# A hybrid mixer: one half of a convolution a step later, a gate product in its old place, and three small sums further back on VectorE

## The chip, the cores and the metric

The kernel runs on one core of a Trainium2 chip. The metric is the device time of one execution in microseconds (us). Three timed executions of the kernel before gave 1531.76, 1535.86 and 1537.22 us; their median, 1535.86 us, is the time before. The profiled execution took 1536.88 us, of which the span from the first to the last instruction is 1535.1 us.

## The reference

The network has two layers over 128 context tokens and 256 latent tokens of width 1024. Each layer is a half-step SwiGLU network, a token mixer, and a second half-step SwiGLU network, each with adaptive shift, scale and gate and a layer norm behind it. The mixer has one input projection and one output projection, and between them three head groups side by side:

```python
z = h @ p["w_in"]
zq, zi, zff, zfb, zg, zglu, cq, ck, cv = jnp.split(z, cuts, axis=-1)
o_fw, s_fw = _hgrn_scan(qa, k_fw, ia, logf_fw, s0[:, 0])            # linear recurrence, forward
o_bw, s_bw = _hgrn_scan(rev(qa), rev(k_bw), rev(ia), rev(logf_bw), s0[:, 1])
o_a = _rms_norm(o_fw + rev(o_bw), g) * jax.nn.silu(zg)              # gated by zg
u = _depthwise_conv(glu_a * jax.nn.sigmoid(glu_b), conv_w, conv_b)  # 31 taps, 256 channels
o_conv = jax.nn.silu(_layer_norm(u, conv_ln_g, conv_ln_b))
kc = _rms_norm(ck, p["k_norm_g"])                                   # keys, then rotary for latents
o_c = _block_attention(qc, kc, vc)
y = jnp.concatenate([o_a, o_conv, o_c], axis=-1) @ p["w_out"]
```

All of it is fp32. The change touches three things of the mixer: the depthwise convolution, the product that gives `zg`, and the sums of squares in the keys' RMS norm.

## The kernel before, in words

The 384 tokens are three blocks (`tok` 0 is the context, 1 and 2 are the latents). The order of instructions on TensorE (PE), VectorE (DVE), ScalarE (ACT) and GpSimd (POOL) is the order in which the Python code is written (`manual_schedule`); each engine works its own list in order and waits at an instruction whose input is not there. There is no planner around the change; DMAs are issued by SyncE (SP), in order too.

The change lies in the loop `for i in range(2 * NT + 1)` of `mixer` (seven steps, `i` = 0 to 6), which runs once a layer. Its pieces are these:

- `scores(i)`: 64 small matmuls (32x32 and 64x64 tiles, L1195) for one pair of heads and one token block, into one of two PSUM pairs, and then four masked copies on VectorE (`copy_predicated`, L1204) that put them into the tiles `A1[i % 2]` and `A2[i % 2]`.
- `outputs(i - 1)`: the matmuls that read those tiles (L1229). For token blocks 1 and 2 two groups on carried states come first; then the group on `A2`, which needs the second masked copy, and then the group on `A1`, which needs the fourth.
- `conv(ct)`: half of the channels of the convolution, 32 matmuls in the code and 64 records in the trace (L1004), and ScalarE's evacuation (L1012). `CONV_AT` says at which step each half stands.
- `zg(n)`: the gate's projection for one token block, 24 matmuls of 128x256 (L664) from `W[14]` and `W[15]`, and a ScalarE copy. `HFILL` says at which step the first one stands; the other two stand in the attention loop behind.
- In step 0, `prep(14)` and `prep(15)` split two weight tiles (ScalarE cast L888, VectorE subtraction L894). In steps 0 and 1, `dec[1].level(32)` and `level(64)` work on decay tiles (L1118 to L1125).
- `head_ssq` (L931 to L938): a ScalarE square, a VectorE sum (L932) and two GpSimd instructions; three calls for the keys, whose result is read by `norm_rope` (L948 to L956) in steps 2, 3 and 4.
- In step 4, behind the second half of the convolution, `wo_prep(4)` and `wo_prep(5)` split weights of the output projection (L600, L601). In step 6 `keys_turn` transposes the keys (L1420), after `norm_rope` of token block 2, and `att(0)` begins the attention (L1445).

Of the kernel before, what the change touches and what calls it, by code (L numbers as in the profile page):

```python
# [18 lines left out]
P = 128  # L19
DM = 1024  # L20
KT = 8
NT = 3
# [11 lines left out]
]  # L34
NA = len(ATT_ORDER)
UW, UC, OW = 432, 428, 399
CONV_AT = {2: 0, 4: 1}
MH = 4
TMID = 2
FILL = (-1, 1, 2)  # L40
HFILL = (5,)
SLOW, FAST, LAST = [2, 2, 2, 2], [3, 2, 3], [3, 3, 1, 1]


class Net:
# [810 lines left out]
    def mixer(self, l, eps, nxt):  # L856
# [12 lines left out]
        mp = scope(es, "mix")  # L869
# [29 lines left out]
        def prep(n, eng, pool=None):  # L899
            lo(n, hi(n, pool))  # L900
# [11 lines left out]
        kn = self.t(mp, [P, NT, P], "kn")  # L912
# [14 lines left out]
        def head_ssq(x, nh, t1):  # L927

            f = 64 if nh == 8 else 1
            ss = self.t(mp, [P, 16], "ss", bufs=8)  # L930
            nc.scalar.activation(t1, x, AF.Square)  # L931
            nc.vector.reduce_sum(  # L932
                ss[:, 0:nh], t1.rearrange("p (h d) -> p h d", d=64), axis=AX.X
            )
            nc.gpsimd.tensor_scalar(
                ss[:, 0:nh], ss[:, 0:nh], f / 64, f * 1e-6, ALU.mult, ALU.add
            )
            nc.gpsimd.tensor_tensor(  # L938
                ss[:, 8 : 8 + nh], ss[:, 0:nh], self.eps[:, 2:3].to_broadcast([P, nh]), ALU.pow
            )  # L940
            return ss
# [191 lines left out]
        def state_turn(p):  # L1133
            pt = self.wbank()
            for i, (d, tok) in enumerate(((0, 0), (0, 1), (1, 0), (1, 2))):
                nc.tensor.transpose(
                    pt[:, i * P : (i + 1) * P],
                    dec[p].Kc[d][:, tok * P : (tok + 1) * P],
                    self.ident,
                )  # L1140
            kN = self.t(hp, [P, 4, P], "kN")
            nc.scalar.copy(kN.rearrange("p a b -> p (a b)"), pt)
            return kN

        def states(p, kN):
            pt = self.wbank()
            for i, tok in enumerate((0, 1, 0, 2)):
                for hh in range(2):
                    rs = slice(64 * hh, 64 * hh + 64)
                    nc.tensor.matmul(  # L1150
                        pt[rs, i * 64 : i * 64 + 64],
                        kN[:, i, rs],
                        vN[:, tok, 128 * p + 64 * hh : 128 * p + 64 * hh + 64],
                        start=True,
                        stop=True,
                    )
            S1 = self.t(hp, [P, 4, 64], "S1", bufs=2)
            for i, d in ((0, 0), (2, 1)):
                nc.scalar.copy(S1[:, i, :], pt[:, i * 64 : i * 64 + 64])
                nc.sync.dma_start(  # L1160
                    self.o["new_state_hgrn"][0, l, d, 2 * p : 2 * p + 2].rearrange(
                        "h d e -> (h d) e"
                    ),
                    S1[:, i, :],
                )
            for i, d in ((1, 0), (3, 1)):
                nc.vector.scalar_tensor_tensor(
                    S1[:, i, :], S0[:, d, p, :], dec[p].et[d][:, d + 1 : d + 2],
                    pt[:, i * 64 : i * 64 + 64], ALU.mult, ALU.add,
                )  # L1170
            return S1
# [3 lines left out]
        def scores(i):  # L1175

            p, tok = divmod(i, NT)
            Qd, Kd, lev = dec[p].D, dec[p].K, dec[p].lev  # L1180
            tsl = slice(tok * P, (tok + 1) * P)
            a1, a2 = A1[i % 2], A2[i % 2]
            prs = [(Qd[0], Kd[0], a1), (Qd[1], Kd[1], a2)] + [(q_, k_, a1) for q_, k_ in lev]
            if i < 2:
                sbs[i] = self.pair(1 + i)
            sb = sbs[i % 2]
            for kd_, m, x in ((0, 32, 0), (1, 32, 0), (2, 32, 0), (3, 32, 0), (4, 32, 32), (5, 64, 64)):
                n = min(kd_, 3)
                if i < 2 and n < 3:
                    m = P  # L1190
                for hh in range(2):
                    rs = slice(64 * hh, 64 * hh + 64)
                    for c in range(0, P, m):
                        r = c ^ x
                        nc.tensor.matmul(  # L1195
                            sb[c : c + m, hh, n * P + r : n * P + r + m],
                            prs[kd_][1][rs, tok * P + c : tok * P + c + m],
                            prs[kd_][0][rs, tok * P + r : tok * P + r + m],
                            start=True,
                            stop=True,  # L1200
                            tile_position=(64 * hh, c),
                        )
            for n in range(4):
                nc.vector.copy_predicated(  # L1204
                    prs[n][2],
                    self.smask[:, n, :].unsqueeze(1).to_broadcast([P, 2, P]),
                    sb[:, :, n * P : (n + 1) * P],
                )
# [141 lines left out]
        k_ss = []  # L1350
# [35 lines left out]
        glu(1)  # L1386
        S1s = [states(0, kN)]
        dec[1].level(16)
        for tok in range(NT):
            k_ss.append(head_ssq(kn[:, tok, :], 2, self.t(mp, [P, P], "t1k", bufs=2)))  # L1390
        nc.sync.dma_start(self.o["new_cache_v"][0, l].rearrange("s h d -> s (h d)"), kv[:, 0, :])

        wop, wraw = {}, {}
# [2 lines left out]
        def wo_load(kb):  # L1396
            raw = wraw[kb] = self.t(self.rawp, [P, 2, DM], "raw")
            if kb < 4:
                nc.sync.dma_start(
                    raw, wo[l, kb * P : (kb + 2) * P, :].rearrange("(k p) n -> p k n", p=P)  # L1400
                )
            else:
                for g in range(2):
                    r0 = 512 + g * 256 + (kb - 4) * 64
                    nc.sync.dma_start(
                        raw[64 * g : 64 * g + 64],
                        wo[l, r0 : r0 + 128, :].rearrange("(j p) n -> p j n", p=64),
                    )

        def wo_prep(k, pool, tag, size=2 * DM, lo=nc.vector):  # L1410
            w = self.t(pool, [P, size], tag, F32R)[:, 0 : 2 * DM]
            w = w.rearrange("p (a n) -> p a n", a=2)
            wop[k] = self.split_to(w, wraw[k // 2 * 2][:, k % 2, :], lo)
# [3 lines left out]
        def keys_turn():  # L1417
            pt = self.wbank()
            for i, src in enumerate((kn[:, 0, :], ck[:, 0, :], kn[:, 1, :], kn[:, 2, :])):
                nc.tensor.transpose(pt[:, i * P : (i + 1) * P], src, self.ident)  # L1420
            nc.scalar.copy(kT.rearrange("p a b -> p (a b)"), pt)
# [93 lines left out]
        def att(n):  # L1515
            units.append(Att(n))
            units[n].scores()

        for i in range(2 * NT + 1):
            if i < 2 * NT:  # L1520
                scores(i)
            if i == NT + 1:
                S1s.append(states(1, kN))
            if i == NT:
                kN = state_turn(1)
            if i == 2 * NT:
                keys_turn()
            if i == 0:
                prep(14, nc.vector)
                prep(15, nc.vector)  # L1530
            if i == 2:
                wo_load(4)
            if i in CONV_AT:
                conv(CONV_AT[i])
            if i == 5:
                wo_load(6)
                wo_load(0)
                wo_load(2)
            if i == 4:
                wo_prep(4, self.wgu, "wgu")  # L1540
                wo_prep(5, self.wgu, "wgu")
            if i > 0:
                outputs(i - 1)
            if i in HFILL:
                zg(HFILL.index(i))
            if i == NT + 1:
                o_turn(0)
            if i == 2 * NT:
                att(0)
                units[0].exp()  # L1550
            if i == NT:
                es1.close()
                ap_ = scope(es, "at")
                gh = self.t(ap_, [P, 1, 256], "gh")
                nc.sync.dma_start(
                    gh[:, 0, :], a["hgrn_norm_g"][l : l + 1, :].to_broadcast([P, 256])
                )
            if i < 2:
                dec[1].level(32 << i)
            elif i < 2 + NT:  # L1560
                tok = i - 2
                norm_rope(
                    kn[:, tok, :], k_ss[tok], tok, 2, 1, self.t(mp, [P, P], "t1k", bufs=2)
                )
# [233 lines left out]
```

## Time and profile before

| what | value |
|---|---|
| median of three timed executions | 1535.86 us |
| profiled execution, its own time | 1536.88 us |
| span of the profiled execution | 1535.1 us |
| TensorE matmuls busy | 1508.9 us (98%) |
| VectorE, ScalarE, GpSimd busy | 1058.8, 649.2, 59.2 us |
| mean granted TensorE clock | 0.993 |

Busy times are of one engine each and overlap. A busy TensorE says that matmuls are in flight, not that they run at their best pace; the granted clock says how much of the full 2.4 GHz the engine got. The chain of waits walks back from the last instruction to whatever released it, so its pieces add up to the span, where the busy times do not.

### The profile page before, as it was taken

To read this page: it belongs to the slowest core of one execution; us is meant where nothing else is said; L and a number is where in the kernel's file an instruction comes from. 1 tells how busy PE (TensorE), PEld (TensorE's weight loads), DVE (VectorE), ACT (ScalarE), POOL (GpSimd) and SP (SyncE) were. 2 spreads that over 40 slices of the span, in tenths; PEclk is the share of its full clock that TensorE was granted. 3 is DMA by queue.
4 is the path that set the end of the run, shared out by engine and by line. 5 is a ranking of instruction groups with operands and counts; after the bars stand their busy time and mean duration, and the time that the engine had idled before them with its cause. 6 is when DMAs were issued, how large, how long until landed. Compare 5 with 4: busy or idle time off the path is not lost.

```text
span 1535.1 us, 23662 instructions
## 1 busy us (share of the span) xinstructions
PE 1508.9 (98%) x9605; PEld 1343.1 (87%) x9605; DVE 1058.8 (69%) x1525; ACT 649.2 (42%) x1112; POOL 59.2 (4%) x96
## 2 busy tenths in 40 slices
PE   8999999999999999999999999999999999999997
PEld 7889999989677899999989999998986789999996
DVE  4788878679667777777676676675795786554334
ACT  3434333367475533333353333333773764332331
POOL 0000000030101000000000000000210100000001
PEclk9999999999999999999999999999999999999998
DMA  9886766423524466666535565642335146342411
GB/s 385 307 292 227 243 233 222 176 67 134 125 83 165 165 225 230 231 221 211 201 114 216 168 244 192 220 164 112 118 102 160 48 168 248 127 179 110 165 55 41
DMA packets 63940, 272.27 MB, mean 177 GB/s; under 512 B 9224, under 2 KB 13784, under 8 KB 48984
## 3 DMA queue, kind: packets, MB, share of 16 engines
q1 hardware_dynamic: 63832, 270.77, 49.8%
q8 instruction: 75, 1.23, 0.3%
q14 instruction: 33, 0.27, 0.1%
HBM read 267.71 MB, written 3.03 MB: 176 GB/s over the span
## 4 chain that ended last, share of the span: by engine, by line
PE 92%; ACT 2%; DVE 2%; DMA 2%; issue 1%; SPq 0%; POOL 0%; DVEq 0%; POOLq 0%; ACTq 0%
PE w L610 45%; PE d L623 26%; PE d L683 7%; PE d L610 4%; PE w L1004 2%; PE w L664 1%; PE w L208 1%; PE d L1195 1%; PE w L427 1%; PE d L1229 1%; ACT Pr L1463 1%; DVE G L196 1%; PE d L1445 1%; PE d L1493 1%; DMA wi<-ffn_w_in_first 1%
## 5 line engine op out<-in xcount | busy, mean ns | idle before, releaser
L610 PE MATMUL w<-xh,wgu 128*128 128x384 f32 x2720 | 711.6, 337 | 1.4 <-DVE hf L777 1.4
L610 PEld LDWEIGHTS w<-xh,wgu 128*128 128x128 f32 x2720 | 494.0, 188 | 10.9 <-issue 4.9
L610 PE MATMUL w<-xl,wgu 128*128 128x384 f32 x1360 | 455.7, 335 | 0.0
L623 PE MATMUL d<-wo,hh 128*128 128x512 f32 x1056 | 284.4, 391 | 1.5 <-DVE hf L777 1.5
L196 DVE SCALAR_TENSOR_TENSOR G<-t,cc,G 128x1024 f32<-128x1024 f32 x224 | 272.9, 1280 | 0.0
L610 PEld LDWEIGHTS w<-xl,wgu 128*128 128x128 f32 x1360 | 256.3, 188 | 2.2
L623 PEld LDWEIGHTS d<-wo,hh 128*128 128x128 f32 x1056 | 196.8, 188 | 38.4 <-DVE hf L777 1.9
L601 DVE TENSOR_TENSOR wgu<-raw,wgu 128x1024 fp32r<-128x1024 f32 x166 | 196.1, 1222 | 39.1 <-ACT wgu L600 38.6
L779 ACT CAST hh<-hf 128x384 fp32r<-128x384 f32 x82 | 42.1, 514 | 343.4 <-DVE hf L777 343.4
L777 DVE TENSOR_TENSOR hf<-w,sg 128x384 f32<-128x384 f32 x79 | 44.0, 557 | 182.6 <-PE w L610 182.6
L600 ACT CAST wgu<-raw 128x1024 fp32r<-128x1024 f32 x166 | 166.2, 1049 | 3.4 <-DMA raw<-ffn_w_in 3.4
L623 PE MATMUL d<-wo,hl 128*128 128x512 f32 x528 | 163.2, 390 | 0.0
L775 ACT ACTIVATE sg<-w 128x384 f32<-128x384 f32 x79 | 38.8, 491 | 264.2 <-PE w L610 264.2
L623 PEld LDWEIGHTS d<-wo,hl 128*128 128x128 f32 x528 | 99.1, 188 | 21.2
L601 DVE TENSOR_TENSOR wo<-raw,wo 128x1024 fp32r<-128x1024 f32 x90 | 109.7, 1219 | 10.9 <-ACT wo L600 10.9
L683 PE MATMUL d<-wgu,xh 128*128 128x512 f32 x336 | 104.6, 392 | 0.0
L600 ACT CAST wo<-raw 128x1024 fp32r<-128x1024 f32 x90 | 94.4, 1049 | 11.7 <-DMA raw<-ffn_w_out 11.3
L780 DVE TENSOR_TENSOR hl<-hf,hh 128x384 fp32r<-128x384 f32 x82 | 45.8, 559 | 47.6 <-ACT hh L779 47.6
L683 PEld LDWEIGHTS d<-wgu,xh 128*128 128x128 f32 x336 | 62.3, 188 | 12.5
L683 PE MATMUL d<-wgu,xl 128*128 128x512 f32 x168 | 65.6, 390 | 0.0
L436 ACT ACTIVATE t<-w,colB,colA 128x128 f32<-128x128 f32 x120 | 43.6, 469 | 46.3 <-PE w L427 38.7
L486 POOL TENSOR_TENSOR st<-st,eps 128x1 f32<-128x1 f32 x18 | 8.0, 445 | 1202.0 <-ACT X L482 1202.0
(279 smaller groups left out, 1513.7 us busy)
## 6 DMA issues: line engine op xcount, KB each, us to landing
raw<-ffn_w_in SPq DMA_DIRECT2D x80, 1024.0 KB
t<-w_mod SPq DMA_DIRECT2D x128, 512.0 KB
raw<-ffn_w_out SPq DMA_DIRECT2D x44, 1024.0 KB
raw<-w_in SPq DMA_DIRECT2D x12, 1024.0 KB
raw<-entry SPq DMA_DIRECT2D x10, 1024.0 KB
raw<-w_mod_first SPq DMA_DIRECT2D x8, 1024.0 KB
G<-gates SPq DMA_DIRECT2D x12, 512.0 KB
raw<-w_in_vk SPq DMA_DIRECT2D x4, 1024.0 KB
```

Source lines behind the costliest of these rows:

```text
L196: nc.vector.scalar_tensor_tensor(ac, raw, cc, ac, ALU.mult, ALU.add)
L436: self.nc.scalar.activation(m[:, k, :], pts[k // 4][:, k % 4 * P : (k % 4 + 1) * P], AF.Identity, scale=A[:, k, c : c + 1], bias=B[:, k, c ...
L600: nc.scalar.copy(w[:, 0], src)
L601: lo_engine.tensor_tensor(w[:, 1], src, w[:, 0].bitcast(F32), ALU.subtract)
L610: nc.tensor.matmul(ps, w[:, wi, k, :], x[:, k, :], start=(k == 0 and i == 0), stop=(k == KT - 1 and i == 2),)
L623: nc.tensor.matmul(acc[:, n, :], h, w[:, wi, n * 512 : n * 512 + 512], start=(first and i == 0), stop=(last and i == 2),)
L683: self.nc.tensor.matmul(ps, x[:, k, tok * P : (tok + 1) * P], w[k // 2][:, wi, k % 2, :], start=(k == 0 and i == 0), stop=(k == KT - 1 and ...
L775: nc.scalar.activation(sg, pg, AF.Silu)
L777: nc.vector.tensor_mul(hf, pu, sg)
L779: nc.scalar.copy(hh, hf)
L780: nc.vector.tensor_sub(hl, hf, hh.bitcast(F32))
L1004: nc.tensor.matmul(pc_[32 * j : 32 * j + 32, :], cw[:, ct, j, m, :], U[ct][:, j, 4 * m : 4 * m + OW], start=(m == 0), stop=(m == 7), tile_ ...
```

## The change

Three edits. The first half of the convolution moves from step 2 to step 3. The first gate product moves from step 5 to step 2, where it stands behind `outputs(1)`. The three `head_ssq` calls for the keys move from before the loop to step 1, behind `scores(1)` with its masked copies and behind `level(64)`.

```diff
-CONV_AT = {2: 0, 4: 1}
+CONV_AT = {3: 0, 4: 1}
-HFILL = (5,)
+HFILL = (2,)
@@
         dec[1].level(16)
-        for tok in range(NT):
-            k_ss.append(head_ssq(kn[:, tok, :], 2, self.t(mp, [P, P], "t1k", bufs=2)))
@@
             if i < 2:
                 dec[1].level(32 << i)
+                for tok in range(NT if i else 0):
+                    k_ss.append(head_ssq(kn[:, tok, :], 2, self.t(mp, [P, P], "t1k", bufs=2)))
```

No instruction is added or taken away on any engine. SyncE's list of DMAs keeps its order.

TensorE before, from the end of `scores(2)` to the beginning of `scores(3)` (`db` and `sk` hold decayed queries and keys, `da` queries, `S` states, `A` the masked score tiles, `raw` the convolution's blocks and shifted inputs):

```order
L1195 MATMUL d_496_3602<-db_3155 64x64 x4
L1004 MATMUL w_505_3749<-raw_3500,raw_3453 32x399 x32
L1229 MATMUL d_495_3601<-da_3154,S_433_3140 64x128 x2
L1229 MATMUL d_495_3601<-da_3154,S_486_3563 64x128 x2
L1229 MATMUL d_495_3601<-A_437_3148,vN_2910 64x128 x2
L1229 MATMUL d_495_3601<-A_436_3147,vN_2910 64x128 x2
L1195 MATMUL d_501_3651<-sk_2983 32x32 x16
```

The same place on TensorE in the changed kernel, as far as the gate product's first matmuls (`wgu` is `W[14]`):

```order
L1195 MATMUL d_490_3584<-db_3155 64x64 x4
L1229 MATMUL d_489_3583<-da_3154,S_433_3140 64x128 x2
L1229 MATMUL d_489_3583<-da_3154,S_486_3563 64x128 x2
L1229 MATMUL d_489_3583<-A_437_3148,vN_2910 64x128 x2
L1229 MATMUL d_489_3583<-A_436_3147,vN_2910 64x128 x2
L664 MATMUL w_505_3757<-wgu_3615,xh_117 128x256 x2
L664 MATMUL w_505_3757<-wgu_3615,xl_118 128x256
```

The convolution no longer stands between `scores(2)` and `outputs(1)`; the gate product stands behind `outputs(1)`.

VectorE at the beginning of the loop, the difference (`t1k` is a square of a key block; `A_434` and `A_435` are the tiles of `scores(0)`):

```order
-L932 TENSOR_REDUCE ss_3583<-t1k_3582 128x2
-L932 TENSOR_REDUCE ss_3589<-t1k_3588 128x2
-L932 TENSOR_REDUCE ss_3595<-t1k_3594 128x2
-L1204 COPY_PREDICATED A_434_3143<-smask_1094,d_496_3602 128x256
-L1204 COPY_PREDICATED A_435_3144<-smask_1094,d_496_3602 128x256
-L1204 COPY_PREDICATED A_434_3143<-smask_1094,d_496_3602 128x256 x2
-L894 TENSOR_TENSOR wgu_3633<-raw_3234,wgu_3633 128x1024
-L894 TENSOR_TENSOR wgu_3636<-raw_3234,wgu_3636 128x1024
+L1204 COPY_PREDICATED A_434_3143<-smask_1094,d_490_3584 128x256
+L1204 COPY_PREDICATED A_435_3144<-smask_1094,d_490_3584 128x256
+L1204 COPY_PREDICATED A_434_3143<-smask_1094,d_490_3584 128x256 x2
```

The three sums are gone from the place ahead of the masked copies of `scores(0)`. The two weight subtractions and `level(32)` still stand between those copies and the copies of `scores(1)`.

TensorE in the changed kernel from the end of `outputs(4)` to the first scores of the attention (`kn` the keys, `ck` the cached keys; L1418 and L1443 are L1420 and L1445 of before):

```order
L1229 MATMUL d_489_3583<-A_434_3143,vN_2910 64x128 x2
L1418 MATMUL w_523_4078<-ident_91,kn_2912 128x128
L1418 MATMUL w_523_4078<-ident_91,ck_2915 128x128
L1418 MATMUL w_523_4078<-ident_91,kn_2912 128x128 x2
L1229 MATMUL d_489_3583<-da_3160,S_514_3953 64x128 x2
L1229 MATMUL d_489_3583<-da_3160,S_433_3140 64x128 x2
L1229 MATMUL d_489_3583<-A_437_3148,vN_2910 64x128 x2
L1229 MATMUL d_489_3583<-A_436_3147,vN_2910 64x128 x2
L1443 MATMUL d_524_4093<-kT_2917,qT_2916 128x384 x2
```

Before, the 24 matmuls of the gate product stood between the first of these rows and the second.

## Rows read from the trace of the kernel before

**Rows 1.** The page, parts 1 and 4: busy times; the chain by engine.
```profile
PE 1508.9 (98%) x9605; PEld 1343.1 (87%) x9605; DVE 1058.8 (69%) x1525; ACT 649.2 (42%) x1112; POOL 59.2 (4%) x96
...
PE 92%; ACT 2%; DVE 2%; DMA 2%; issue 1%; SPq 0%; POOL 0%; DVEq 0%; POOLq 0%; ACTq 0%
```

**Rows 2.** Chain of waits, layer 0's loop: start, us, what held the end.
```profile
393.64 0.62 PE w L1150 x16
394.25 2.91 PE d L1195 x98
...
399.22 1.09 PE d L1195 x62
400.30 0.39 issue
...
401.16 6.93 PE w L1004 x64
408.09 1.17 PE d L1229 x16
...
410.36 0.59 PE w L1136 x4
...
414.18 5.50 PE w L1004 x64
419.67 0.59 PE d L1229 x8
...
422.86 3.07 PE w L664 x24
...
427.54 0.85 PE d L1445 x4
```

**Rows 3.** Chain of waits, layer 1's loop.
```profile
1142.49 0.62 PE w L1150 x16
...
1160.42 1.44 issue
1161.86 7.20 PE w L1004 x64
1169.06 0.59 PE d L1229 x8
```

**Rows 4.** Timeline, layer 0: start, us, instruction, [idle before <- releaser].
```profile
396.29 0.47 DVE L932 TENSOR_REDUCE ss<-t1k 128x2 f32<-128x128 f32 x2
...
397.15 1.58 DVE L1204 COPY_PREDICATED A<-smask,d 128x256 f32<-128x256 uint8 x4
...
397.96 0.44 PE L1229 MATMUL d<-A,vN 128*64 128x128 f32 x4 [0.84 <-DVE A L1204]
...
398.62 2.35 DVE L894 TENSOR_TENSOR wgu<-raw,wgu 128x1024 fp32r<-128x1024 f32 x2
...
398.78 0.44 PE L1229 MATMUL d<-A,vN 128*64 128x128 f32 x4 [0.38 <-DVE A L1204]
...
402.12 1.58 DVE L1204 COPY_PREDICATED A<-smask,d 128x256 f32<-128x256 uint8 x4
```

**Rows 5.** Stretches: us, PE, PEld, DVE, ACT, POOL busy, PEclk (granted clock), DMA, GB/s.
```profile
50.00:51.00 1.00, 0.00 (x0) 0.00 (x0) 1.00 (x2) 0.00 (x0) 0.00 (x0) 1.00 0.22 86
...
400.50:400.75 0.25, 0.06 (x1) 0.06 (x2) 0.25 (x1) 0.00 (x0) 0.25 (x1) 0.76 0.60 151
...
1161.75:1162.00 0.25, 0.14 (x4) 0.17 (x8) 0.17 (x1) 0.00 (x0) 0.00 (x0) 0.61 0.04 7
```

**Rows 6.** Timeline, layer 0, behind the convolution's second half.
```profile
419.74 0.59 ACT L1012 ACTIVATE ua<-w,pcol 128x399 f32<-128x399 f32 x1 [5.19 <-PE w L1004]
...
424.88 0.29 DVE L956 TENSOR_TENSOR kn<-kn,t1k 128x128 f32<-128x128 f32 x1
...
425.08 1.58 DVE L1204 COPY_PREDICATED A<-smask,d 128x256 f32<-128x256 uint8 x4
```

**Rows 7.** Chain of waits, layer 0, in the attention behind.
```profile
437.67 1.78 ACT Pr L1463 x8
```

## The prediction

> **What bounds the kernel now.** I read the page first: TensorE is busy 98% of the span, and 92% of the chain that ended last is its matmuls [rows 1]. So the question is how long TensorE stands or crawls in the seven-step loop, once a layer, before and after. I then read the chain of waits over that loop in both layers, and there the reader is to see where pieces other than matmuls stand and which matmul pieces are too long.
>
> Take the stretch from `states(0)` to the end of the convolution's second half, which is the start of `outputs(3)`. In layer 0 it is 419.67 - 393.64 = 26.03 us [rows 2], in layer 1 it is 1169.06 - 1142.49 = 26.57 us [rows 3]. The work in it at full pace: two `states` 2 x 0.62, the first two `scores` 2.91, `outputs(0)` 2 x 0.44, three more `scores` 3 x 1.09, two halves of the convolution 2 x 5.50, two `outputs` 2 x 1.17, one turn 0.59 [rows 2, 4], together 22.23 us. So 3.80 us in layer 0 and 4.34 us in layer 1 are waits and slow clock.
>
> The timeline names the waits. `outputs(0)` waits 0.84 us and then 0.38 us for the masked copies, in both layers alike [rows 4]. Layer 1 has 1.44 us ahead of the second half of the convolution, which the profile puts down to nothing (it is the input's transfer, I suppose), and then 7.20 us where layer 0 took 5.50: 1.70 us lost [rows 3]. In layer 0 it is the first half that is slow, 6.93 instead of 5.50 us: 1.43 us lost, and most of the rest lies just before it, with 0.39 us of "issue" [rows 2]. The stretches explain both: right behind these waits the granted clock falls from its upper level, 2.4 GHz, to its lower one, 1.2 GHz (the two quarters of a microsecond in which it happens have means of 0.76 and 0.61) [rows 5].
>
> **The change part by part.**
>
> *The sums of squares.* Three sums leave the place ahead of the masked copies of `scores(0)`: those copies can start where the first sum stood, 396.29 instead of 397.15, 0.86 us earlier [rows 4]. That takes the 0.84 us wait; the 0.38 us wait is between the second and the fourth copy and stays. VectorE's whole list up to the copies of `scores(1)` comes 0.86 us earlier: these start at 402.12 - 0.86 = 401.26. In their new place the sums (0.47 us for two) delay only the copies of `scores(2)`, which are read behind the convolution, and ScalarE and GpSimd have nothing urgent behind theirs: cost nothing, at most one 0.86 us if that cover is gone.
>
> *The convolution's first half leaves step 2.* Its 5.50 us stood between `scores(2)` and `outputs(1)` and covered the copies of `scores(1)`, which end at 402.12 + 1.58 = 403.70 while TensorE was busy until 408.09 [rows 2, 4]. Without it TensorE has `scores(2)` done at 399.22 + 1.09 - 0.84 = 399.47, and the half of `outputs(1)` on states (0.58 of 1.17) at 400.05. The next group needs the second copy, which is there 0.81 us after their start (397.96 against 397.15), at 402.07: a wait of 2.02 us. After 0.29 us of matmuls the last group needs the fourth copy, 1.63 us after the start (398.78 against 397.15), at 402.89: 0.53 us more. VectorE cannot be sooner: between the two sets of copies stand the weight subtractions of 2.35 us [rows 4] and `level(32)`, all in one list, and TensorE's gate product is queued behind the waiting `outputs(1)`, so nothing fills the wait. New waits: 0.38 + 2.02 + 0.53 = 2.93 us.
>
> *The gate product comes in.* 3.07 us [rows 2] are added ahead of the convolution's end. The stretch becomes 22.23 + 3.07 + 2.93 = 28.23 us: 2.20 us longer than layer 0's and 1.66 us longer than layer 1's, whose transfer wait of 1.44 us is gone because the second half now starts later than its input lands.
>
> *The gate product leaves step 5.* There it stood on TensorE from 422.86 to 425.93 [rows 2], and one would book 3.07 us as won. But ScalarE's evacuation of the second half begins only when that half ends, and behind it in the two lists come the casts, the subtractions and `norm_rope` of token block 2, which ends at 424.88 + 0.29 = 425.17 [rows 6]. The last key transpose needs it. Counted from the end of the convolution (419.67), TensorE runs out of work at 422.86 - 419.67 = 3.19 us, does three of the four transposes, and the keys are there at 5.50 us: about 2.0 us of new wait. The copies of `scores(5)` start at 425.08, or 5.41 us, and their fourth is there at 7.04 us; the attention begins at about 7.42 us instead of 427.54 - 419.67 = 7.87 us [rows 2, 6]. Won: 0.45 us a layer, not 3.07.
>
> Sum at the clock as it was: (2.20 - 0.45) + (1.66 - 0.45) = 1.75 + 1.21 = 3.0 us more. It carries through to the end, since TensorE is the chain.
>
> *The clock.* Each layer now has two waits of about 2 us with small work around them, where before it had 0.84 and 0.38, and in layer 1 1.44. What a wait does to the clock is bounded by rows of both kinds: 1.44 us in layer 1 was followed by the lower clock, and so were 0.84, 0.38 and 0.39 us close together in layer 0; but the same two first waits in layer 1 were not, nor was over 1 us of idle TensorE around 50 us, with the clock at 1.00 [rows 2 to 5]. A fall costs between nothing, where it lies over a wait, and the 1.70 us that [rows 2, 3] show. Longer waits than any of these in the loop make a fall likely at each of the four. I price one at 1.2 us, the lower row 1.43 less some 0.25 that falls on the short second wait, and take three of four: 3.6 us.
>
> The Trainium skill ("TensorE: Matmul & The Clock Gate", section "Loop structure matters more than you think") holds against this that a VectorE copy out of PSUM between tiles, with the next matmuls right behind, "doesn't break PE warmth". By it the four waits, all on VectorE, would leave the clock alone, and the sum would be 3.0 us. The row of layer 0 disagrees, the one of layer 1's first waits agrees; the long waits have no row.
>
> Forecast: 3.0 + 3.6 = 6.6 us on the profiled execution, 1536.88 + 6.6 = 1543.5. That execution lies 1.02 us above the median of the timed ones, so the time is 1542.5 us: slower by 0.43%.
>
> **The rivals.**
>
> *The waits, but no falls.* For it: 50 us and layer 1's first waits. Then 3.0 us: 1535.86 + 3.0 = 1538.8 us. This is also what the rule above gives.
>
> *Slower beyond doubt: a fall at each of the four waits, at the full price.* Its place is the gate product behind `outputs(1)` and the attention's first products behind the keys, both dense work on TensorE directly behind a wait, where each fall takes the 1.70 us of above. 3.0 + 4 x 1.70 = 9.8 us: 1545.6 us. It decides over the forecast from 7.7 us on, that is once the falls cost 4.7 us together.
>
> *Faster: `outputs(1)` finds its copies done.* Then 2.02 + 0.53 us go in each layer: 3.0 - 5.1 = -2.1 us, 1533.8 us. For it only that the sums are out of the way; against it the 4.97 us between the starts of the two sets of copies (402.12 - 397.15), in which TensorE now has less than 3 us of work [rows 2, 4].
>
> *The slip is absorbed.* In the attention the chain runs over ScalarE's exponentials for a while [rows 7]; if it did so regardless of when TensorE begins, nothing would be left: 1535.9 us. Against it, these exponentials wait for TensorE's scores, which the slip moves.
>
> **How the numbers follow.** Less than 0.5% (7.7 us) is about what a measurement of this kernel cannot tell from no change. Chances: forecast 0.40, no falls 0.17, all four 0.30, faster 0.05, absorbed 0.08. The monitor behind the clock is said by the Trainium skill (same page, "What's actually happening") to run free of the kernel's start, so that a change of clock comes at another place in another run. The two layers, alike in work and unlike in where the clock fell, agree with that. Falls of clock will therefore differ from run to run, as the 5.5 us between the three times before may show. The range goes from just below the no-fall case, 1536.8, to the four falls with 1 us over, 1546.6. Beyond 0.5% slower is the case of four falls, 0.30, and the upper part of the forecast's own spread, 0.07: 0.37. Faster by over 0.5% would need nearly all of the 3.80 + 4.34 us that the loop loses now: 0.02. Within: 0.61.
>
> **What would show it.** In the changed profile, in both layers: `outputs(0)` with no first wait; a wait of about 2 us and one of about 0.5 us before `outputs(1)`'s last two groups, on the masked copies; no wait before the convolution's second half; about 2 us of idle TensorE before the last key transpose; and the lower clock behind some of these. From `states(0)` to the attention 28.23 + 7.42 = 35.7 us at full clock, against 33.90 (427.54 - 393.64) in layer 0. The prediction is wrong if the copies of `scores(1)` are early, if the gate product fills their wait, or if the keys no longer hang on the convolution's end.

## The result: 0.8% slower

Four timed executions of the changed kernel took 1544.22 to 1548.70 us, median 1548.32 us, against 1535.46 us for four of the kernel before. The ratio is 1.0082, its 95% interval 1.0065 to 1.0098. The forecast was 1542.5 us: the direction was right, and the time lies above the range. The profiled execution is the lowest of the four, 1544.22 us with a span of 1542.4 us, so each step below is read in the trace and its size in the timed runs as well.

From the page after, the two lines that answer to [rows 1]:

```profile
PE 1510.2 (98%) x9605; PEld 1345.5 (87%) x9605; DVE 1058.8 (69%) x1525; ACT 649.3 (42%) x1112; POOL 55.9 (4%) x96
...
PE 91%; ACT 3%; DVE 3%; DMA 2%; issue 1%; SPq 0%; POOL 0%; DVEq 0%; POOLq 0%; ACTq 0%
```

TensorE is as busy as before within 1.3 us; the chain has more VectorE and ScalarE. Where these stand is in the chain of waits after, in layer 0's loop (start, us, what held the end), which answers to [rows 2]; the last four lines are of layer 1:

```profile
391.38 0.64 PE w L1150 x16
...
399.08 1.03 DVE A L1204 x3
...
400.63 0.63 PE d L1229 x4
401.26 4.37 PE w L664 x24
405.62 1.08 PE d L1195 x61
406.70 1.25 issue
...
424.37 2.36 DVE wgu L601 x2
...
428.23 1.03 DVE A L1204 x3
...
430.22 0.84 PE d L1443 x4
...
1154.84 4.56 PE w L664 x24
...
1182.24 0.58 PE d L1229 x4
1182.82 1.58 PE d L1443 x4
1184.40 3.71 PE w L664 x24
```

The masked copies (L1204) hold `outputs(1)`; the gate product (L664) takes 4.37 us, in layer 1 4.56 us, instead of 3.07; 1.25 us of "issue" stand near the end of `scores(3)`; and behind the second half of the convolution the chain runs over the weight subtractions, the keys and the last copies. The waits themselves are in the timeline of TensorE after: in layer 0 the one wait that `outputs(0)` has left, a stop and a wait in step 2, and the wait for the keys; then all of layer 1's:

```profile
395.67 0.44 PE L1229 MATMUL d<-A,vN 128*64 128x128 f32 x4 [0.38 <-DVE A L1204]
399.10 0.27 PE L1195 MATMUL d<-db 64*64 64x64 f32 x1 [1.91 <-issue]
400.63 0.63 PE L1229 MATMUL d<-A,vN 128*64 128x128 f32 x4 [0.37 <-DVE A L1204]
...
428.29 0.33 PE L1418 MATMUL w<-ident,kn 128*128 128x128 f32 x1 [1.88 <-DVE kn L956]
...
1149.44 0.44 PE L1229 MATMUL d<-A,vN 128*64 128x128 f32 x4 [0.38 <-DVE A L1204]
...
1153.60 0.44 PE L1229 MATMUL d<-A,vN 128*64 128x128 f32 x4 [2.19 <-DVE A L1204]
1154.40 0.44 PE L1229 MATMUL d<-A,vN 128*64 128x128 f32 x4 [0.37 <-DVE A L1204]
1180.74 0.33 PE L1418 MATMUL w<-ident,kn 128*128 128x128 f32 x1 [1.89 <-DVE kn L956]
1182.24 0.58 PE L1229 MATMUL d<-A,vN 128*64 128x128 f32 x4 [0.21 <-DVE A L1204]
```

The first wait of [rows 4], 0.84 us, is gone and 0.38 stays. The forecast waits are there: 2.19 and 0.37 us for 2.02 and 0.53, and 1.88 and 1.89 us before the last key transpose for 2.0. In layer 0 the wait of 2.19 us is not seen: a stop of 1.91 us that the profile puts down to nothing stands in its time. Then the clock, in windows after (columns as in [rows 5]):

```profile
403.00:403.50 0.50, 0.50 (x5) 0.50 (x4) 0.50 (x2) 0.00 (x0) 0.33 (x3) 0.50 1.01 221
404.00:404.50 0.50, 0.50 (x5) 0.50 (x5) 0.47 (x3) 0.00 (x0) 0.33 (x3) 0.84 1.10 213
1156.50:1157.00 0.50, 0.50 (x4) 0.50 (x4) 0.50 (x3) 0.00 (x0) 0.42 (x2) 0.50 0.91 197
1184.00:1184.50 0.50, 0.50 (x3) 0.17 (x2) 0.05 (x1) 0.00 (x0) 0.00 (x0) 0.50 1.27 523
430.00:430.50 0.50, 0.50 (x6) 0.30 (x4) 0.00 (x0) 0.23 (x1) 0.00 (x0) 1.00 1.00 401
```

Both gate products run in part at 1.2 GHz (a granted clock of 0.50), and layer 1's first attention product does as well; layer 0's runs at 2.4 GHz. Three of the four waits had a fall behind them in this execution. From `states(0)` to the attention the loop takes 430.22 - 391.38 = 38.84 us (33.90 before) and 37.67 us in layer 1 (34.44 before).

**A way to split every timed run.** Each run gives its span and the mean granted clock. One minus that clock, times the span, is counted as lost to the lower clock; the time less this is called the rest. The clock is given to three digits, so one run's split is good to 0.8 us. It also counts a lower clock that lies over a wait, where it costs little, so "lost" is an upper figure and "rest" a lower one. Over 91 runs of the kernel before, the means are: time 1534.7 us, lost 8.4, rest 1526.25. Over ten of the kernel after: time 1548.7 us, lost 14.2, rest 1534.4. So of 14.0 us, 5.8 are clock and 8.2 are waits and stops, each with a standard error of 0.6 to 0.9 us, for the ten runs scatter. The two profiled executions do not show this: they lost 10.7 us (before) and 10.8 us (after), the one more than its kernel's mean and the other less.

### The profile page after: what moved, and what is told of

Read it like the earlier page. It is cut to its first block, busy times and chain, and to the rows that moved or that the text cites. A ratio compares the mean times of both kernels' runs of the same rounds, so it can differ in the third digit from the quotient of the medians.

```text
span 1542.4 us, 23665 instructions
## 1 busy us (share of the span) xinstructions
PE 1510.2 (98%) x9605; PEld 1345.5 (87%) x9605; DVE 1058.8 (69%) x1525; ACT 649.3 (42%) x1112; POOL 55.9 (4%) x96
## 4 chain that ended last, share of the span: by engine, by line
PE 91%; ACT 3%; DVE 3%; DMA 2%; issue 1%; SPq 0%; POOL 0%; DVEq 0%; POOLq 0%; ACTq 0%
PE w L610 45%; PE d L623 26%; PE d L683 7%; PE d L610 4%; PE w L1004 1%; PE w L664 1%; PE w L208 1%; PE w L427 1%; ACT wgu L600 1%; ACT Pr L1461 1%; PE d L1443 1%; DVE G L196 1%; PE d L1491 1%; DMA raw<-w_mod_first 1%; PE w L1480 1%
## 5 line engine op out<-in xcount | busy, mean ns | idle before, releaser
L610 PE MATMUL d<-xh,wgu 128*128 128x384 f32 x192 | 51.4, 339 | 0.3 <-ACT wgu L600 0.3
```

What stands on the lines that cost most here:

```text
L610: nc.tensor.matmul(ps, w[:, wi, k, :], x[:, k, :], start=(k == 0 and i == 0), stop=(k == KT - 1 and i == 2),)
```

## The experiments

The theory (A): the loss is TensorE's new waits, and the falls of clock behind them. The rivals are: the unexplained "issue" stops are fetches of TensorE's own instructions and cost by themselves (C); or, for the 1.44 us of layer 1, the convolution's input transfer (T); or the new order of TensorE's list costs something without its waits. The table is in the order of the text. The time is a median, "lost" and "rest" are means; "ratio" is to runs of the kernel before beside it on the same chip, whose medians were 1534.16 to 1534.83 us.

| kernel | median us (runs) | ratio, 95% interval | lost to clock | rest |
|---|---|---|---|---|
| sums_only | 1535.09 (12) | 1.0004, 0.9993 to 1.0015 | 8.7 | 1526.5 |
| conv_only | 1538.92 (12) | 1.0030, 1.0019 to 1.0041 | 12.9 | 1525.9 |
| gate_only | 1542.01 (6) | 1.0047, 1.0030 to 1.0065 | 12.3 | 1529.9 |
| gate_first | 1540.00 (10) | 1.0035, 1.0021 to 1.0048 | 11.1 | 1529.0 |
| before_fewer | 1533.12 (12) | 0.9994, 0.9982 to 1.0005 | 7.3 | 1526.3 |
| sums_fewer | 1532.51 (12) | 0.9992, 0.9981 to 1.0004 | 7.5 | 1526.1 |
| sums_fewest | 1535.08 (12) | 1.0006, 0.9994 to 1.0018 | 8.1 | 1527.5 |
| after_fewer | 1545.76 (6) | 1.0080, 1.0066 to 1.0094 | 14.4 | 1531.9 |
| one_load | 1537.18 (12) | 1.0008, 0.9998 to 1.0017 | 10.1 | 1526.5 |
| after_busy | 1550.02 (4) | 1.0114, 1.0098 to 1.0129 | 11.6 | 1539.4 |
| after_busy2 | 1548.00 (6) | 1.0079, 1.0065 to 1.0092 | 9.8 | 1538.1 |
| after_rep | 1548.28 (6) | 1.0091, 1.0077 to 1.0106 | 14.7 | 1534.8 |
| keys_cover | 1541.73 (7) | 1.0042, 1.0027 to 1.0057 | 11.4 | 1529.6 |
| both_cover | 1531.80 (12) | 0.9980, 0.9969 to 0.9991 | 7.0 | 1524.6 |

**One part of the change alone.** `sums_only`: the `head_ssq` lines alone.

> Only the three sums of the keys' squares move; convolution and gate product stay. Theory A (waits on masked copies, on the keys, and the falls of clock behind them): outputs(0) loses its first wait of 0.84 us in each layer, nothing else waits; 1535.5 - 1.7 = 1533.8 us, and 1 to 2 us less still if the fall of clock in layer 0 goes with the wait. Rival B (the sums in their new place hold up VectorE and are part of the loss): 0.9 us a layer or more on top, 1537 us or above. Rival C (stops of TensorE that the trace calls issue, with a fetch of instructions just before them, set by how many instructions stand ahead): the stops before the convolution's halves stay where they are in the order, 0.4 us in layer 0 and about 1.4 us in layer 1.

No difference is seen, where (A) alone gave 1533.8 us. The 0.84 us wait is gone, but the stops grew: 1.27 us for 0.39 in layer 0, and 1.91 for 1.44 in layer 1. TensorE came earlier to a place where it was stopped anyway.

`conv_only`:

```diff
-CONV_AT = {2: 0, 4: 1}
+CONV_AT = {3: 0, 4: 1}
```

> Only the convolution's first half moves to step 3; the gate product stays in step 5 and the sums stay ahead. Theory A: outputs(1) waits about 2.0 and 0.5 us for the copies of scores(1) in each layer, the keys are still covered by the gate product; the loop keeps its length at full clock (2.5 us of new wait against 0.9 to 1.4 us of old stops that go), a fall at the wait in each layer: 1535.5 + 2 to 4 = 1538 to 1539.5 us. Rival B (the convolution's place is all of the loss): 1546 to 1548 us, as the changed kernel.

The time is as (A) expects, the waits are not: in the profile they are 0.62 us in layer 0, behind a stop of 1.24, and 1.29 us in layer 1, where the clock is at 0.50 before and through the wait. By the split nearly all of the loss is clock: the rest is 0.4 us below that of before, and 4.5 us more are lost. A part of these lies over the wait and so belongs to the rest.

`gate_only`:

```diff
-HFILL = (5,)
+HFILL = (2,)
```

> Only the gate product moves to step 2, behind outputs(1); the convolution's first half stays in step 2 ahead of it and covers the masked copies; the sums stay ahead. Theory A: no wait at outputs(1); about 2 us of wait before the last key transpose in each layer, 0.45 us won there at full clock, the gate product's 3 us paid ahead of the convolution's end: +2.6 us in layer 0; in layer 1 the 1.44 us ahead of the second half were the input's transfer and go, with the fall behind them: about 0; plus falls at the keys: 1535.5 + 3 to 6 = 1538.5 to 1541.5 us. Rival C: the 1.44 us of layer 1 are a fetch of instructions and not a transfer; the stop is still there, moved by the 24 matmuls that now stand earlier, or at another place of the loop.

A little above the range. Both layers wait 1.88 us for the last key transpose, together 3.8 us; the rest is longer by 3.6 us, and 3.9 us more go to the clock.

**The gate product over one wait.** `gate_first` is the changed kernel with two blocks swapped:

```diff
+            if i in HFILL:
+                zg(HFILL.index(i))
             if i > 0:
                 outputs(i - 1)
-            if i in HFILL:
-                zg(HFILL.index(i))
```

> The changed kernel with the gate product of step 2 put ahead of outputs(1) instead of behind it, so that it stands where the convolution stood. Theory A: the 3.07 us of the gate product cover the copies of scores(1), the waits of 2.0 and 0.5 us go from both layers (unless the weight splits, done just before, hold it), the falls behind them go too; the waits at the keys stay: 1548.3 - 5 to 8 = 1540 to 1543 us. Rival B (the copies were not the cause): 1546 us or more.

As expected, 8.3 us below the changed kernel: the rest is shorter by 5.4 us, where two waits of 2.19 + 0.37 us are 5.1. TensorE's waits in its layer 1, from the timeline, are the one that `outputs(0)` has left, the keys' and the last copies':

```profile
1152.88 0.44 PE L1229 MATMUL d<-A,vN 128*64 128x128 f32 x4 [0.37 <-DVE A L1204]
1179.74 0.33 PE L1418 MATMUL w<-ident,kn 128*128 128x128 f32 x1 [1.88 <-DVE kn L956]
1181.24 0.44 PE L1229 MATMUL d<-A,vN 128*64 128x128 f32 x4 [0.21 <-DVE A L1204]
```

**What the "issue" stops are.** `before_fewer` leaves out 15 of 27 warming matmuls, whose result nobody reads and which all stand in the first 15 us of the program; nothing in the loops or in the DMAs differs.

```diff
-            self.setup(lambda: warm(9))
-            warm(6)
+            self.setup(lambda: warm(4))
+            warm(4)
...
-            warm(4)
+            warm(2)
...
-            warm(2)
...
-            warm(6)
+            warm(2)
```

> The kernel before with 15 of the 27 warming matmuls at the program's start left out (their result is read by nobody), so that every later instruction of TensorE stands 15 matmuls (30 records) earlier in its list. Theory C (stops at fixed places of the list, where the next piece of instructions has not been fetched): the stop of 0.39 us inside scores(2) of layer 0 and the 1.46 us ahead of the convolution's second half in layer 1 fall some 30 records later, into the convolution's slow matmuls, and vanish or shrink, with the falls of clock behind them: the loops 33.9 and 34.4 us become 32.4 to 33 us each, 1534.2 - 2 to 4 = 1530 to 1532 us. Rival T (the 1.46 us are the wait for the convolution input's transfer): 1.46 us stay in layer 1, the loop 34.4 us, 1534 us. The start of the program may lose or win up to 1 us.

The loops took 32.26 and 31.27 us for 33.90 and 34.44, with neither stop; a new one of 0.66 us stands at layer 0's second `states`. Its chain in layer 1, against [rows 3]:

```profile
1139.71 0.62 PE w L1149 x16
...
1157.00 0.62 PE w L1149 x16
1157.61 5.50 PE w L1003 x64
1163.11 0.59 PE d L1228 x8
```

TensorE reaches the second half of the convolution 17.90 us after `states(0)`, as it did before (1160.42 - 1142.49 = 17.93), and finds its input there. So (T) falls. What moved is the place in TensorE's list at which the next packet of its instructions was due. The trace has 75 such packets of 16 KB, on a queue of their own; one lies just ahead of the stop of [rows 3], in the DMA view of the kernel before from 1158.90 to 1160.35 us (queue, packets, MB, share):

```profile
q8 instruction: 1, 0.02, 5.7%
```

By the trace's records it ended at 1160.29, and TensorE went on at 1161.86. After the change one ended at 406.24, and TensorE went on at 407.95.

The traces of all the runs show what sets the place. TensorE has 9605 matmuls and 9605 weight loads, and 75 packets for these 19210 records are about 256 a packet. Counted along TensorE's list of matmuls and weight loads, all 37 stops of 0.15 us and more that the profile puts down to nothing, past the first 100 us of the 16 traces of this case, stand 193 to 195 records behind a multiple of 256, in whatever piece of the loop that is, and each 1.2 to 1.7 us behind the end of a packet. (C) is thus shown for where the stops stand; why a packet comes late there is not. For the time `before_fewer` gives less than expected: the median is 1.7 us lower, above the 1530 to 1532 us, and the interval holds 1.

`sums_fewer` and `sums_fewest` are `sums_only` with 15 and 21 of the warming matmuls left out.

> Only the sums moved, with the same 15 warming matmuls left out. Theory C: what the sums won in front of outputs(0), 0.84 us a layer, was taken back by the stops behind (0.39 to 1.27 us in layer 0, 1.46 to 1.91 in layer 1); without these stops it is won: 0.8 us a layer under the kernel before with fewer warming matmuls, 1529 to 1530.5 us. Rival: no difference between the two (the 0.84 us is lost elsewhere).

> The sums moved and 21 instead of 15 warming matmuls left out: every place where a fetch can stop TensorE falls another 12 records later than in the run with 15 left out. Theory C: the 1.34 us at the states of layer 0 move into the convolution's second half and shrink, the 0.79 us of layer 1 move behind scores(5): 1530.5 to 1532 us, the least of all. Rival (the stops find another place as bad): 1532.5 us as with 15 left out, or more.

Neither is told from the kernel before, and both miss what (C) gave for the time. In `sums_fewer` stops of 1.34 and 0.79 us stand in the loops; in `sums_fewest` stops of 1.06, 0.47 and 0.39 us turned up at other places, and one of 1.76 us ahead of the convolution's first half that the profile puts down to a transfer. Leaving out instructions moves the stops; it does not abolish them.

`after_fewer` leaves the same 15 out of the changed kernel.

> The changed kernel with the same 15 warming matmuls left out. Theory C: the stop of 1.25 us inside scores(3) of layer 0 falls into the convolution's first half and goes, the waits on the masked copies (2.0 to 2.2 and 0.4 us) and on the keys (1.9 us) stay: 1548.3 - 1.3 to 2.5 = 1546 to 1547 us; the difference to the kernel before with fewer warming matmuls is then larger than 13 us. Rival A alone (no fetches): unchanged within 0.5 us but for the start.

The 1.25 us stop went, a short one of 0.31 came, the waits stayed at 2.19, 0.37 and 1.89 us: the rest is 2.5 us shorter, and the clock loses as much as ever, 14.4 us. So stops are a small part of the loss, 2.5 of 14 us.

`one_load` gives the second half of the convolution the first half's input (that input is not written and loaded, so half of the convolution is not the reference's).

> The kernel before without the second half's transfers of the convolution's input (one write and four scattered loads a layer); its matmuls read the first half's input instead, so this part of the result is not computed. Theory C with a cause (the fetch of instructions comes late because it stands behind the scattered loads of the convolution's input on the DMA engines): the stop ahead of the second half in layer 1, 1.46 us, goes; the one of 0.39 us in layer 0, which stands behind the first half's loads, stays; 1531 to 1533 us. Rival (the fetch is late whatever the loads do, for it is asked for late): 1.46 us stay. Rival T (the 1.46 us are the transfer itself): they go and no fetch lies before the place; the fetch's packet then tells the two apart, since it must come earlier here if the loads held it.

The time missed, 1537.18 us for 1531 to 1533. Layer 0's stop stayed, 0.52 us. Layer 1's was gone, but there the lower clock held TensorE back until the packet had come, so this run does not decide between (C) and (T); `before_fewer` and the count of records do.

**Dummy products in the waits.** `after_busy` puts 7 narrow matmuls, `after_busy2` 2 wide ones, into each of the four long waits:

```diff
+                if i == 1 and k == n - 2:
+                    keep(2)
...
+                if i == 3:
+                    keep(2)
```

> The changed kernel with 7 extra matmuls of constants (14 records, about 1.9 us at full clock, read by nobody) put ahead of the group of outputs(1) that waits for the masked copies and 7 ahead of the last key transpose, in both layers: TensorE is busy in the waits, which stay as long as they are. Theory A: the clock does not fall behind them, and the time is the changed kernel's less the falls: 1548.3 - 4 to 6 = 1542 to 1544.5 us, 3 to 4 us above the kernel before for the waits alone plus up to 1.3 us for the stop of layer 0. Rival (the falls of clock do not matter, the waits or the gate product's place itself cost 12 us): 1547 us or more.

> The changed kernel with TensorE kept busy in the four waits by 2 wide matmuls each (128x512, 4 records, about 1.7 us at full clock, read by nobody) instead of 7 narrow ones, so that the list of instructions hardly shifts. Theory A: waits and stops as in the changed kernel, but the clock stays up behind the waits: 1548.3 - 4 to 6 = 1542 to 1544 us, with 8 to 9 us lost to the lower clock over the program instead of 13.5. Rival (the falls come from the stops or from elsewhere): 1547 us or more and the lower clock as often as in the changed kernel.

Both missed. The clock did better, 11.6 and 9.8 us lost for 14.2, and in the second one's trace no fall lies behind any of the four waits. But the dummies take their own time, and stops came: 4.37 us in one place of the first, 2.79 and 2.13 us in the second, so the rest grew by 5.0 and 3.6 us. What the filling gave was given back.

`after_rep` is the changed kernel once more.

> The changed kernel once more, for more runs: 1547 to 1549 us, and 13 to 14 us lost to the lower clock on average, against 8.4 us in the kernel before.

The result repeats, and its profiled execution is the slowest of the ten, 1554.30 us, as the first was the fastest. In this profile all four places had a fall, the keys' wait in both layers, where the first profile had one in layer 1 alone; a fifth fall stood behind a stop of 2.15 us. The falls were longer, too: the chain has 7.93 us for a half of the convolution (5.50 at full clock) and 4.84 us for a gate product behind the keys (3.06).

**Real products over the waits.** `keys_cover` moves a second gate product from the attention loop to step 5, and `both_cover` has the swap of `gate_first` as well:

```diff
-FILL = (-1, 1, 2)
-HFILL = (2,)
+FILL = (-1, -2, 2)
+HFILL = (2, 5)
```

> The changed kernel with a second gate product (that of token block 0) taken from the attention loop and put into step 5, where TensorE waited 1.88 us and 0.21 us for the keys and the last copies in each layer. If the time comes from TensorE's waits and the falls of clock behind them: both waits go in both layers, 4.2 us at full clock, and about half of the 5.8 us more that the changed kernel loses to the lower clock: 1541 to 1543 us. If the cost hangs on the gate product's place behind outputs(1) alone: 1548 us still. If the attention's first exponentials are bare without the product that stood beside them: 1544 to 1546.

> The same, with the first gate product also ahead of outputs(1), so that both long waits have a product over them. Waits and falls: only the wait of 0.37 us stays in each layer, the kernel does the work of before at its pace and loses no more than it to the lower clock: 1532.5 to 1536 us. If the place of the gate product is what counts and not the waits: 1540 us, as with the gate product ahead of outputs(1) alone. If the attention's first exponentials are bare: 1536 to 1538.

Both came out as (A) expects, the second a little faster still. By means, the four corners are 1548.7 us (no wait covered), 1540.1 (the ones of `outputs(1)`), 1541.0 (the keys'), 1531.6 (both): 8.6 and 7.7 us alone, 17.0 together. They add within 0.8 us, about their error, and no loss is left that the new place of the convolution as such would have to explain. What the second product's leaving the attention loop does by itself was not run. `both_cover` beats both kernels: its rest lies 1.6 us under that of before, about 2 x 0.84 us, the wait that the sums' move takes away. TensorE's waits in its layer 1, from the timeline, are one:

```profile
1145.86 0.44 PE L1229 MATMUL d<-A,vN 128*64 128x128 f32 x4 [0.38 <-DVE A L1204]
```

## Why the prediction had the direction and not the size

- *The waits were right.* By its own terms they come to 2.93 new, 1.22 gone, 3.07 for the gate product and 0.45 won: 4.33 us a layer, 8.7 us for two. The rests of the timed runs differ by 8.2 us. The loops agree: 38.84 less the 1.25 us stop and 1.49 us of slow clock (4.37 + 0.63 against 3.07 + 0.44) is 36.1 us, and 37.67 less 1.49 and 0.14 us of slow clock is 36.0 us in layer 1, for 35.7 forecast.
- *The step that failed is the clock's term: 3.6 us for three falls, set beside a "sum at the clock as it was" of 3.0 us.* That sum takes a changed stretch at full pace less a stretch of before that held falls of 1.43 and 1.70 us, 3.1 together, and 2.6 us of stops and odds [rows 2, 3]: 8.7 - 3.1 - 2.6 = 3.0. So the old falls were booked as won in full, and with 3.6 us for three new ones the clock came to + 0.5 us net. It measured + 5.8 us over the timed runs. One profiled execution was no measure of what there was to win: it lost 10.7 us to the clock, where 91 runs of its kernel lost 8.4 on average.
- *The price of a fall was too low as well.* Three of four waits had one in the first profile, as taken, but its rows give 1.49 us behind each gate product (4.37 + 0.63 against 3.07 + 0.44, and 4.56 against 3.07) and 1.53 behind layer 1's keys (0.58, 1.58 and 3.71 for 0.44, 0.84 and 3.06 us), not 1.2; and in `after_rep` single pieces of work lost 2.4 and 1.8 us. The prediction says that the long waits have no row. The trace of before had one: at 87.00 us, ahead of L208, TensorE had been idle for 2.54 us, and the granted clock was 0.50 from there to 93.00.
- *The 1.44 us were no transfer.* They were a stop that moves with the list, and one came back as 1.25 us in `scores(3)`, a term that the sum did not have. By the rests, the runs show 0.5 us of the 2.6 as won.
- *The sum on one profiled execution came near by luck:* 7.3 us of span for 6.6 forecast. From the first loop on that execution was 9.6 us longer than the one before, but it began that loop 2.3 us sooner (391.38 against 393.64), in a part that the change does not touch. It is also the fastest of the ten.
- *The rivals.* Four falls at 1.70, 1545.6 us, was nearest and also too low, from the same base. Falls of clock behind the waits, not their absence, are what the runs show, so the no-fall rival fails. The sentence of the Trainium skill ("TensorE: Matmul & The Clock Gate", "Loop structure matters more than you think") that a VectorE copy out of PSUM "doesn't break PE warmth" is about matmuls that follow immediately, and was stretched to cover these waits: here TensorE stood for 2.19 us on such copies, and for 1.89 us on keys that are no copy out of PSUM, and 1.2 GHz followed. That the monitor runs free of the kernel's start (same page, "What's actually happening") agrees with the keys' wait of layer 0, 1.88 us in two executions of one kernel, with a fall in one and none in the other.

What stays open: which single wait a fall belongs to. In `conv_only` 4.5 us more went to the clock with waits of 0.62 and 1.29 us, and layer 1's fall came in its profile ahead of the 1.29. The dummies and the covers show the tie of falls to waits only for means over runs.

## What to carry to other kernels

Before a changed stretch at full pace is compared with the old one, take the old one's slow clock and unexplained stops out too, unless something in the change removes them. One profiled execution is a poor measure of what the clock takes: over ten runs of one kernel it took from 10.8 to 20.2 us. The waits on a saturated TensorE cost 1.7 to 1.8 times their length here (8.6 us for 5.1 us of waits, 7.7 for 4.2), and were removed by real work already there in the list's neighbourhood, not by dummy work.

## What the hardware showed that was not expected

TensorE stops inside runs of small matmuls or right behind them, on no semaphore, and goes on 1.2 to 1.7 us past the end of a 16 KB packet of its own instructions; the 37 stops counted here lasted from 0.18 to 4.37 us. The place is set by the number of instructions ahead of it: every one stood at the same count of records within a packet's 256. 15 matmuls fewer at the program's start took both old stops out of the loops and brought a shorter one, and 21 fewer brought others. A gain ahead of such a place is lost in it, as in `sums_only`.

The Trainium skill ("Runtime: NRT & Kernel Launch", section "Instruction fetch mechanics") says that instructions are refilled in 16 KiB blocks and calls the cost of crossing one "mostly hidden". The packets of 16 KB agree with it; the cost does not in runs of short matmuls, where a stop ends behind a packet.
